# Projections with stationary weights: the high parts of two units, the low parts of all four, the high parts of the other two

## The chip, the cores and the metric

One Trainium2 chip, one NeuronCore of it. The metric is the device time of one execution in microseconds (us). Three runs of the kernel before gave 1080.13 us in the median (1079.92 to 1081.16).

## What is computed

One decoder layer on 256 tokens of width 2048, in float32. A combined input projection feeds 16 heads of sliding-window attention (window 128, two key/value heads, ALiBi, a learned sink per head) and 16 heads of forgetting attention ("FoX": the logit gets c[t] - c[s], where c is the running sum of log-sigmoid gates). Each group is RMS-normalised, one output projection follows, then a gated MLP with a causal convolution of width 3.

```python
h = rmsnorm(x, pre_mix_g)
q_a, k_a, v_a, q_b, k_b, v_b, f_b = split(h @ w_in)
o_a = swa_sink_attention(q_a, k_a, v_a, sinks)
o_b = forgetting_attention(q_b, k_b, v_b, log_sigmoid(f_b + b_forget))
x = x + rmsnorm(concat(rmsnorm(o_a), rmsnorm(o_b)) @ w_out, post_mix_g)
h = rmsnorm(x, pre_ffn_g)
gate, val = split(causal_dwconv(h @ w_up, conv_w, conv_b))
x = x + rmsnorm((gelu(gate) * val) @ w_down, post_ffn_g)
```

## The kernel before

Every float32 operand of a large product is split in two: a high part rounded to the matmul's float32r format and a low part with the rest. High x high, low x high and high x low are accumulated in PSUM. Weights come from HBM in units of 128 x 1024 numbers (512 KB). `w_load` starts the DMA into a tile `raw`, `w_split` has ScalarE (ACT) copy it into `whi` (line 111) and VectorE (DVE) subtract into `wlo` (line 114). `raw`, `whi` and `wlo` have five buffers each.

`proj_T` computes 256 output columns, transposed, with the weights stationary. The moving operand `hT` holds per row block the high part of the activations in columns 0 to 255 and the low part in 256 to 511. A high product (line 252) multiplies a 128 x 128 piece of `whi` with all 512 columns; a low product (line 257) multiplies a piece of `wlo` with the 256 high columns. The contraction of 2048 is 16 steps `kt`, four to a unit; each step is two products, one for each of the two PSUM banks. It is used 54 times: 3 times for queries of the sliding window, 8 times for queries and keys of FoX, 43 times in the MLP. Before, it takes the units in two passes of two: seven steps of high products, eight of low ones, the eighth of high ones.

TensorE's (PE's) instructions stand in the order of the code; a scheduler orders the other engines, whose queues run strictly in that order. The attention is woven into the projections by a clock of its own: `tick()` raises a counter and runs what `later(n, f)` had set for that count. `proj_T` ticks eight times; the value projections tick 12 times per block of columns, the output projection twice per unit. `attend` sets four pieces per pair of heads: `tables` (GpSimd, called POOL, fills the tile `p` with the bias), `scores` (12 products, line 441; DVE adds the bias and finds the minimum, line 447, ACT takes the exponential, line 459, DVE takes a reciprocal, line 463, and scales, line 466), `transposes` (6, line 476; ACT writes `ph`, DVE `pl`, lines 278 and 279), and `pv` with the weighted sum (lines 500 and 502 for FoX). They come at the ticks of

```python
def stages(n):
    return n, n + 6, n + 9
```

behind the call: for a FoX group `g` of two pairs, after its projection of queries and its projection of keys, `stages(3 + 8 * m)` for m = 0, 1. PSUM's eight banks are four of tag `acc` for projections and four of tag `att` for the attention. A pair's scores take two `att` banks, its transposes two, its weighted sum one. `p` has two buffers; `ph` and `pl` have one each. Keys of three pairs are kept.

Of the kernel before, what the change touches and what calls it, by code (L numbers as in the profile page):

```python
# [17 lines left out]
P = 128  # L18
# [4 lines left out]
KT = D // P  # L23
# [7 lines left out]
def hybrid_layer(ctx: ExitStack, tc: tile.TileContext, x, pre_mix_g, w_in, b_forget, sinks,  # L31
# [3 lines left out]
    pe, act, dve, pool, sp = nc.tensor, nc.scalar, nc.vector, nc.gpsimd, nc.sync  # L35
# [18 lines left out]
    def tick():  # L54
        now[0] += 1
        for f in todo.pop(now[0], []):
            f()
# [8 lines left out]
    def w_load(src, a, c, pin=False):  # L66
        raw = wp.tile([P, UNIT], F32, tag="raw", bufs=5, name="raw")
        i = sp.dma_start(raw[:, :a * c].rearrange("p (a c) -> p a c", a=a), src)
        if pin:
            tc.keep_in_program_order(i)  # L70
        return raw, a, c
# [4 lines left out]
    def w_parts(n, keep=None, still=False):  # L76


        if keep and keep[0] is None:
            return keep[1]  # L80
        if keep:
            return [keep[0].tile([P, UNIT], F32R, tag="h" + x, bufs=keep[1], name="w" + x)[:, :n]
                    for x in ("hi", "lo")]
        hi = wp.tile([P, UNIT], F32R, tag="whi", bufs=WB, name="whi")
        lo = wp.tile([P, UNIT + 128], F32R, tag="wlo", bufs=WB, name="wlo")
        c = LOW if still else 0
        return [hi[:, :n], lo[:, c:c + n]]
# [13 lines left out]
    def w_split(unit, pin=False, keep=None, begun=None, between=None, still=False):  # L101

        raw, a, c = unit
        n = a * c
        hi, lo = begun or w_parts(n, keep, still)
        for i in range(2 if between else 1):
            cs = slice(i * 512, i * 512 + 512) if between else slice(0, n)
            if i:
                between()
            if not between or i:  # L110
                i1 = act.copy(hi[:, cs], raw[:, cs])  # L111
                if pin:
                    tc.keep_in_program_order(i1)
            i2 = dve.tensor_tensor(lo[:, cs], raw[:, cs], hi[:, cs].bitcast(F32), op=ALU.subtract)  # L114
            if pin:
                tc.keep_in_program_order(i2)
        return [x.rearrange("p (a c) -> p a c", a=a) for x in (hi, lo)]
# [4 lines left out]
    def w_rows(w, k0, a, c0, c):  # L122
        return w[k0 * P:(k0 + a) * P, c0:c0 + c].rearrange("(a p) c -> p a c", p=P)
# [61 lines left out]
    hT = main.tile([P, KT, 512], F32R, tag="hT", name="hT")  # L185
# [55 lines left out]

    def proj_T(w, c0, banks):

        for v in (0, 2):
            parts = [w_split(w_load(w_rows(w, u * 4, 4, c0, 256), 4, 256), still=True)
                     for u in (v, v + 1)]
            steps = [(u, a) for u in range(2) for a in range(4)]

            def high(u, a):
                kt = (v + u) * 4 + a  # L250
                for m, b in enumerate(banks):
                    pe.matmul(b, parts[u][0][:, a, m * P:(m + 1) * P], hT[:, kt, :],  # L252
                              start=(kt == 0), stop=(kt == KT - 1))

            def low(u, a):
                for m, b in enumerate(banks):
                    pe.matmul(b[:, 256:512], parts[u][1][:, a, m * P:(m + 1) * P],  # L257
                              hT[:, (v + u) * 4 + a, 0:256], start=False, stop=False)

            for n, (u, a) in enumerate(steps[:-1]):  # L260
                high(u, a)
                if n in (2, 5):
                    tick()
            for n, (u, a) in enumerate(steps):
                low(u, a)
                if n == 4:
                    tick()
            high(*steps[-1])
            tick()

    def mm3(b, lhs, t, hi, lo, cols, first, last):

# [8 lines left out]
    with tc.tile_pool(name="mixp", bufs=1) as mp:  # L281
# [10 lines left out]
        def x_part(c, k2s, tag="att"):  # L292
            srcs = []
            for k2 in k2s:
                for j in range(2):
                    if tag == "acc" or j == 0:
                        tb = bank(tag)
                    kt = c * 4 + k2 * 2 + j
                    for t in range(2):
                        pe.transpose(tb[:, j * 256 + t * P:j * 256 + (t + 1) * P],  # L300
                                     x_in[:, t, kt * P:(kt + 1) * P], ident)
                    srcs.append((kt, tb[:, j * 256:(j + 1) * 256]))
            to_T(srcs, 0, 256, 0, True)
# [32 lines left out]
        for u in range(4):  # L336
            if u:
                parts = w_split(first[0][u], True, still=True)
            else:
                parts = w_split(first[0][u], True, begun=begun,  # L340
                                between=lambda: x_part(0, (1,), "acc"))
# [5 lines left out]
            parts = w_split(first[1][u], True, still=True)  # L347
# [238 lines left out]
        for g in range(4):  # L586
            if g == 0:
                b2 = bq0
            else:
                b2 = [bank(), bank()]  # L590
                proj_T(w_in, g * 256, b2)
            for m in range(2):
                swa_pair(2 * g + m, q_pair(b2[m]), stages(6 + 8 * (2 * g + m) - 8 * g))
# [3 lines left out]
        for p0, npair, cols in ((0, 3, 384), (3, 3, 384), (6, 2, 272)):  # L597
            b2 = [bank(), bank()]
            c0 = 3328 + p0 * P
            per = 3 if cols == 272 else 2  # L600
            for k0 in range(0, KT, per):
                na = min(per, KT - k0)
                hi, lo = w_unit(w_rows(w_in, k0, na, c0, cols), na, cols)
                for a in range(na):
                    kt = k0 + a
# [48 lines left out]
        for g in range(4):  # L654
            bq = [bank(), bank()]
            proj_T(w_in, 1280 + g * 256, bq)
            qs = [q_pair(b) for b in bq]
            bk = [bank(), bank()]
            proj_T(w_in, 2304 + g * 256, bk)
            for m in range(2):  # L660
                ki = (2 * g + m + 2) % NK
                k_pair(bk[m], ki)
                fox_pair(2 * g + m, qs[m], ki, stages(3 + 8 * m))
# [46 lines left out]
        hT = hT2  # L710
# [101 lines left out]
    with tc.tile_pool(name="ffn", bufs=1) as fp:  # L812
# [89 lines left out]
        for half in range(2):  # L902
            G = [fp.tile([P, 512], F32R, tag="G", bufs=FHALF, name=f"G{j}") for j in range(FHALF)]
            for g in range(FHALF // 2):
                c0 = (half * (FHALF // 2) + g) * 256
# [53 lines left out]
        def before_last(t, n):  # L959

            st = small.tile([P, 1], F32, tag="st", name="st_y")
            dve.tensor_reduce(st, ysq[t][:, 0:n], axis=AX.X, op=ALU.add)
            v = small.tile([P, 1], F32, tag="rv", name="rv")
            dve.tensor_scalar(v, st, 1.0 / D, EPS, op0=ALU.mult, op1=ALU.add)
            return v
# [32 lines left out]
        v = before_last(0, 3)  # L998
# [5 lines left out]
        for h in range(2):  # L1004
            if h:
                v = before_last(1, 4)
# [36 lines left out]
```

## Time and profile before

| | |
|---|---|
| time, median of 3 runs | 1080.13 us |
| the profiled execution: time, span | 1079.4 us, 1077.6 us |
| PE busy | 1064.9 us (99%) |
| DVE busy | 743.8 us (69%) |
| ACT busy | 619.4 us (57%) |
| POOL busy | 180.5 us (17%) |
| read from HBM | 199.58 MB, 187 GB/s with what is written |

The page gives busy time by engine over the whole span. Matmuls overlap in PE's pipeline, so one of 512 columns is listed with 392 ns, while its successor starts earlier; the distance between two starts says what one costs. A share of the whole run hides the stages; the stretch of one stage is read from the busy time by window.

### The profile page before, as it was taken

Reading aid. Unit: us, or ns where it says so; the run is one execution under the profiler, and the core shown is the slowest. Engines: PE = TensorE matmul, PEld = TensorE weight load, DVE = VectorE, ACT = ScalarE, POOL = GpSimd, SP = SyncE. Lnnn points to the kernel's source line nnn. Section 1 sums busy time; section 2 is a strip of 40 time slices with the busy share of each in tenths; the row PEclk is TensorE's granted clock in tenths of the full one; section 3 lists DMA queues with packets and bytes.
Section 4 is the critical chain, followed back from the end, with each engine's and each line's share of the span. In section 5 each row is a group of like instructions: output and inputs, shape, how many; then the busy total and the mean of one; then the engine's idle time right before and its main releaser. Section 6 shows DMA issues by size and latency. Waiting matters only on the chain.

```text
span 1077.6 us, 16247 instructions
## 1 busy us (share of the span) xinstructions
PE 1064.9 (99%) x5986; PEld 926.9 (86%) x5986; DVE 743.8 (69%) x1200; ACT 619.4 (57%) x1060; POOL 180.5 (17%) x252
## 2 busy tenths in 40 slices
PE   9999999999999999999999999999999999999996
PEld 7899988887889888888888888888888888888886
DVE  5988878887568876777677444457777777765563
ACT  7766766667557755656565443456565555644450
POOL 3343244332022201101010000001010100101111
PEclk9999999999999999999999999999999999999999
DMA  8645556544863765555665666665556656565652
GB/s 294 209 120 172 176 171 207 159 149 156 300 227 112 235 193 192 194 189 186 194 193 180 200 197 191 195 192 190 186 192 193 193 182 195 188 198 193 193 166 78
DMA packets 164970, 202.88 MB, mean 188 GB/s; under 512 B 6780, under 2 KB 130972, under 8 KB 164380
## 3 DMA queue, kind: packets, MB, share of 16 engines
q1 hardware_dynamic: 164176, 201.27, 58.3%
q8 instruction: 47, 0.77, 0.3%
q10 hardware_dynamic: 716, 0.58, 0.2%
q14 instruction: 31, 0.25, 0.1%
HBM read 199.58 MB, written 2.11 MB: 187 GB/s over the span
## 4 chain that ended last, share of the span: by engine, by line
PE 89%; DVE 4%; ACT 2%; POOL 2%; issue 2%; DMA 2%; SPq 0%; POOLq 0%; DVEq 0%; ACTq 0%
PE bank_acc L275 34%; PE bank_acc L252 19%; PE bank_att L252 14%; PE bank_acc L257 10%; PE bank_att L257 7%; DVE wlo L114 2%; POOL scr L408 1%; PE bank_att L441 1%; PE bank_acc L881 1%; ACT p L459 1%; PE bank_att L476 1%; DMA x_in<-in_x_dram 1%; PE bank_acc L877 0%; ACT whi L111 0%; DMA c_dram<-scr 0%
## 5 line engine op out<-in xcount | busy, mean ns | idle before, releaser
L114 DVE TENSOR_TENSOR wlo<-raw,whi 128x1024 fp32r<-128x1024 f32 (+3 forms) x357 | 454.2, 1275 | 246.8 <-ACT whi L111 173.6
L111 ACT CAST whi<-raw 128x1024 fp32r<-128x1024 f32 (+3 forms) x356 | 367.9, 1035 | 182.2 <-PE bank_acc L275 117.4
L252 PE MATMUL bank_acc<-hT,whi 128*128 128x512 f32 x1088 | 266.9, 392 | 0.0
L252 PEld LDWEIGHTS bank_acc<-hT,whi 128*128 128x128 f32 x1088 | 198.2, 188 | 37.3
L275 PE MATMUL bank_acc<-whi,G 128*128 128x512 f32 (+1 forms) x724 | 214.5, 378 | 0.0
L275 PEld LDWEIGHTS bank_acc<-whi,G 128*128 128x128 f32 x724 | 133.8, 188 | 25.6
L252 PE MATMUL bank_att<-hT,whi 128*128 128x512 f32 x640 | 154.2, 391 | 0.0
L848 POOL TENSOR_TENSOR u<-u,rowf 128x256 f32<-128x256 f32 x88 | 55.5, 653 | 538.3 <-DVE u L847 536.0
L257 PEld LDWEIGHTS bank_acc<-hT,wlo 128*128 128x128 f32 x1088 | 138.3, 189 | 5.7
L257 PE MATMUL bank_acc<-hT,wlo 128*128 128x256 f32 x1088 | 141.8, 281 | 0.0
L252 PEld LDWEIGHTS bank_att<-hT,whi 128*128 128x128 f32 x640 | 117.6, 188 | 22.7
L275 PE MATMUL bank_acc<-wlo,G 128*128 128x512 f32 (+1 forms) x362 | 137.1, 379 | 0.0
L257 PEld LDWEIGHTS bank_att<-hT,wlo 128*128 128x128 f32 x640 | 81.0, 189 | 3.1
L275 PE MATMUL bank_acc<-whi,oT 128*128 128x512 f32 (+1 forms) x272 | 82.5, 380 | 0.0
L257 PE MATMUL bank_att<-hT,wlo 128*128 128x256 f32 x640 | 82.0, 281 | 0.0
L275 PEld LDWEIGHTS bank_acc<-wlo,G 128*128 128x128 f32 x362 | 68.1, 188 | 12.7
L275 PEld LDWEIGHTS bank_acc<-whi,oT 128*128 128x128 f32 x272 | 50.2, 188 | 9.3
L275 PE MATMUL bank_acc<-wlo,oT 128*128 128x512 f32 (+1 forms) x136 | 51.2, 377 | 0.0
L275 PE MATMUL bank_acc<-whi,hT 128*128 128x384 f32 (+1 forms) x192 | 47.5, 323 | 0.0
L846 ACT COPY cs<-bank_acc 128x256 f32<-128x256 f32 x48 | 15.9, 372 | 52.2 <-PE bank_acc L252 52.2
L459 ACT ACTIVATE p<-p,nm 128x256 f32<-128x256 f32 (+1 forms) x64 | 28.4, 445 | 26.9 <-DVE nm L447 26.9
L846 ACT COPY cs<-bank_att 128x256 f32<-128x256 f32 x40 | 13.3, 373 | 47.2 <-PE bank_att L252 47.2
(200 smaller groups left out, 1016.4 us busy)
## 6 DMA issues: line engine op xcount, KB each, us to landing
raw<-in_w_up_dram SPq DMA_DIRECT2D x176, 512.0 KB, 3.5
raw<-in_w_down_dram SPq DMA_DIRECT2D x88, 512.0 KB, 4.6
raw<-in_w_in_dram SPq DMA_DIRECT2D x51, 512.0 KB, 4.1
raw<-in_w_out_dram SPq DMA_DIRECT2D x32, 512.0 KB, 4.7
raw<-in_w_in_dram SPq DMA_DIRECT2D x16, 384.0 KB, 3.4
cb<-c_dram SPq DMA_DIRECT2D x8, 256.0 KB, 3.6
x_sb<-in_x_dram SPq DMA_DIRECT2D x2, 1024.0 KB
raw<-in_w_in_dram SPq DMA_DIRECT2D x5, 408.0 KB, 3.2
```

Source lines behind the costliest of these rows:

```text
L111: i1 = act.copy(hi[:, cs], raw[:, cs])
L114: i2 = dve.tensor_tensor(lo[:, cs], raw[:, cs], hi[:, cs].bitcast(F32), op=ALU.subtract)
L252: pe.matmul(b, parts[u][0][:, a, m * P:(m + 1) * P], hT[:, kt, :], start=(kt == 0), stop=(kt == KT - 1))
L257: pe.matmul(b[:, 256:512], parts[u][1][:, a, m * P:(m + 1) * P], hT[:, (v + u) * 4 + a, 0:256], start=False, stop=False)
L275: pe.matmul(b, a, r[:, cols], start=(first and i == 0), stop=(last and i == 2))
L408: pool.tensor_tensor(dst, dst, row, op=ALU.mult)
L441: pe.matmul(sb[e][:, cs], a[r, t * P:(t + 1) * P], b[r, 0:nk], start=(n == 0), stop=(n == 2))
L459: act.activation(p[:, e, cs], p[:, e, cs], AF.Exp, bias=nm[:, t, e:e + 1], scale=-1.0, accum_out=rs[:, t, e:e + 1])
L476: pe.transpose(pb[:, i * P:(i + 1) * P], p[:, e, c:c + P], ident)
L846: act.copy(c, b[:, 256:512])
L848: pool.tensor_tensor(u[:, 2:258], u[:, 2:258], rowf, op=ALU.mult)
L881: pe.matmul(v(b), hi[:, ms], v(hT[:, kt, :]), start=(t == 0 and kt == 0), stop=False)
```

## The change

`proj_T` gets all four units in one pass: the high products of units 0 and 1, the low products of 0 and 1, those of 2 and 3, and the high products of 2 and 3. The loads and splits of units 2 and 3 are written behind the low products of units 0 and 1. It ticks four times, in steps 5 (high), 11 (low), 9 and 15 (high). Nothing else is changed: `stages`, the pools and the callers are as before. Line numbers behind it are 9 higher (2 to 3 inside it).

```diff
@@ -241,32 +241,41 @@
 
     def proj_T(w, c0, banks):
 
-        for v in (0, 2):
-            parts = [w_split(w_load(w_rows(w, u * 4, 4, c0, 256), 4, 256), still=True)
-                     for u in (v, v + 1)]
-            steps = [(u, a) for u in range(2) for a in range(4)]
-
-            def high(u, a):
-                kt = (v + u) * 4 + a
-                for m, b in enumerate(banks):
-                    pe.matmul(b, parts[u][0][:, a, m * P:(m + 1) * P], hT[:, kt, :],
-                              start=(kt == 0), stop=(kt == KT - 1))
-
-            def low(u, a):
-                for m, b in enumerate(banks):
-                    pe.matmul(b[:, 256:512], parts[u][1][:, a, m * P:(m + 1) * P],
-                              hT[:, (v + u) * 4 + a, 0:256], start=False, stop=False)
-
-            for n, (u, a) in enumerate(steps[:-1]):
-                high(u, a)
-                if n in (2, 5):
-                    tick()
-            for n, (u, a) in enumerate(steps):
-                low(u, a)
-                if n == 4:
-                    tick()
-            high(*steps[-1])
-            tick()
+
+        parts = {}
+
+        def get(*us):
+            for u in us:
+                parts[u] = w_split(w_load(w_rows(w, u * 4, 4, c0, 256), 4, 256), still=True)
+
+        def high(kt):
+            u, a = divmod(kt, 4)
+            for m, b in enumerate(banks):
+                pe.matmul(b, parts[u][0][:, a, m * P:(m + 1) * P], hT[:, kt, :],
+                          start=(kt == 0), stop=(kt == KT - 1))
+
+        def low(kt):
+            u, a = divmod(kt, 4)
+            for m, b in enumerate(banks):
+                pe.matmul(b[:, 256:512], parts[u][1][:, a, m * P:(m + 1) * P],
+                          hT[:, kt, 0:256], start=False, stop=False)
+
+        get(0, 1)
+        for kt in range(8):
+            high(kt)
+            if kt == 5:
+                tick()
+        for kt in range(8):
+            low(kt)
+        get(2, 3)
+        for kt in range(8, 16):
+            low(kt)
+            if kt == 11:
+                tick()
+        for kt in range(8, 16):
+            high(kt)
+            if kt in (9, 15):
+                tick()
 
     def mm3(b, lhs, t, hi, lo, cols, first, last):
```

On PE, an MLP projection and its neighbour, before (252 high, 257 low; a row with x16 is 16 products in a row):

```order
L252 MATMUL bank_att<-hT_3638,whi 128x512 x14
L257 MATMUL bank_att<-hT_3638,wlo 128x256 x16
L252 MATMUL bank_att<-hT_3638,whi 128x512 x16
L257 MATMUL bank_att<-hT_3638,wlo 128x256 x16
L252 MATMUL bank_att<-hT_3638,whi 128x512 x16
L257 MATMUL bank_att<-hT_3638,wlo 128x256 x16
L252 MATMUL bank_att<-hT_3638,whi 128x512 x16
L257 MATMUL bank_att<-hT_3638,wlo 128x256 x16
L252 MATMUL bank_att<-hT_3638,whi 128x512 x2
```

and now (254 high, 260 low):

```order
L254 MATMUL bank_att<-hT_3638,whi 128x512 x16
L260 MATMUL bank_att<-hT_3638,wlo 128x256 x32
L254 MATMUL bank_att<-hT_3638,whi 128x512 x32
L260 MATMUL bank_att<-hT_3638,wlo 128x256 x32
L254 MATMUL bank_att<-hT_3638,whi 128x512 x16
```

The step from low to high products stood twice in a projection and stands once.

On PE, in the FoX projections, where pairs of heads are woven in. Before, one pair at a time (the rows begin with the end of one pair's scores; 500 and 502 are a weighted sum, 476 are transposes):

```order
L441 MATMUL bank_att<-keys,qh 128x128 x2
L257 MATMUL bank_acc<-hT,wlo 128x256 x6
L252 MATMUL bank_acc<-hT,whi 128x512 x2
L500 MATMUL bank_att<-ph,vpb 128x512 x2
L500 MATMUL bank_att<-pl,vpb 128x512
L502 MATMUL bank_att<-ph,vpb 128x2x128 x2
L502 MATMUL bank_att<-pl,vpb 128x2x128
L252 MATMUL bank_acc<-hT,whi 128x512 x14
L257 MATMUL bank_acc<-hT,wlo 128x256 x16
L252 MATMUL bank_acc<-hT,whi 128x512 x8
L476 MATMUL bank_att<-ident,p 128x128 x6
L252 MATMUL bank_acc<-hT,whi 128x512 x8
```

Now, one place in the projection of queries of the last group (485 transposes, 450 scores, 12 rows of the run; the second pair's scores begin in the last row):

```order
L254 MATMUL bank_acc<-hT,whi 128x512 x28
L485 MATMUL bank_att<-ident,p 128x128 x12
L254 MATMUL bank_acc<-hT,whi 128x512 x4
L260 MATMUL bank_acc<-hT,wlo 128x256 x32
L254 MATMUL bank_acc<-hT,whi 128x512 x4
L450 MATMUL bank_att<-keys,qh 128x256 x2
L450 MATMUL bank_att<-keys,ql 128x256 x2
L450 MATMUL bank_att<-keys,qh 128x256 x2
L450 MATMUL bank_att<-keys,qh 128x128 x2
L450 MATMUL bank_att<-keys,ql 128x128 x2
L450 MATMUL bank_att<-keys,qh 128x128 x2
L450 MATMUL bank_att<-keys,qh 128x256 x2
```

and a little further in the same projection (the end of the second pair's scores, then 509 and 511, the weighted sums):

```order
L450 MATMUL bank_att<-keys,ql 128x128 x2
L450 MATMUL bank_att<-keys,qh 128x128 x2
L254 MATMUL bank_acc<-hT,whi 128x512 x12
L509 MATMUL bank_att<-ph,vpb 128x512 x2
L509 MATMUL bank_att<-pl,vpb 128x512
L511 MATMUL bank_att<-ph,vpb 128x2x128 x2
L511 MATMUL bank_att<-pl,vpb 128x2x128
L509 MATMUL bank_att<-ph,vpb 128x512 x2
L509 MATMUL bank_att<-pl,vpb 128x512
L511 MATMUL bank_att<-ph,vpb 128x2x128 x2
L511 MATMUL bank_att<-pl,vpb 128x2x128
L254 MATMUL bank_acc<-hT,whi 128x512 x16
```

Two pairs' transposes, scores and weighted sums stand side by side. This is so at three ticks for the transposes and weighted sums and at three for the scores.

On ACT, around one pair's softmax in the FoX stage, before (406 evacuates a projection's bank, 459 are exponentials, 278 writes `keys` and `ph`):

```order
L406 COPY scr<-bank_acc 128x256 x2
L111 CAST whi<-raw 128x1024
L278 CAST keys<-scr 128x256 x2
L278 CAST ph<-bank_att 128x384 x2
L111 CAST whi<-raw 128x1024
L459 ACTIVATE p,rs<-p,nm 128x256 x2
L459 ACTIVATE p,rs<-p,nm 128x128 x2
L111 CAST whi<-raw 128x1024
L511 ACTIVATE oT_126<-bank_att,gcol 64x256
L512 ACTIVATE sqo<-bank_att 64x256
```

and now, at the same place as the PE rows above (468 exponentials, 287 `keys` and `ph`, 415 evacuation):

```order
L111 CAST whi<-raw 128x1024
L287 CAST keys<-scr 128x256 x2
L111 CAST whi<-raw 128x1024
L287 CAST ph<-bank_att 128x384 x2
L111 CAST whi<-raw 128x1024
L468 ACTIVATE p,rs<-p,nm 128x256 x2
L468 ACTIVATE p,rs<-p,nm 128x128 x2
L468 ACTIVATE p,rs<-p,nm 128x256 x2
L468 ACTIVATE p,rs<-p,nm 128x128 x2
L111 CAST whi<-raw 128x1024
L415 COPY scr<-bank_acc 128x256 x2
L287 CAST ph<-bank_att 128x384 x2
```

The first `ph` row is that of one pair, the last that of the other pair whose transposes stood in the same tick; the exponentials of two further pairs, a weight copy and two evacuations stand between them.

## The prediction

> **What bounds the kernel.** I read the page first, then the busy time by stage, then the waits of TensorE.
>
> ```profile
> span 1077.6 us, 16247 instructions
> PE 1064.9 (99%) x5986; PEld 926.9 (86%) x5986; DVE 743.8 (69%) x1200; ACT 619.4 (57%) x1060; POOL 180.5 (17%) x252
> ```
> ```profile
> 72.70:128.50 55.80, 55.80 (x384) 54.11 (x383) 47.68 (x115) 37.52 (x88) 19.53 (x23) 1.00 0.51 157
> 168.80:240.80 72.00, 72.00 (x460) 63.07 (x459) 58.80 (x128) 47.91 (x113) 29.46 (x42) 1.00 0.54 166
> 400.00:500.00 100.00, 100.00 (x581) 88.38 (x579) 72.94 (x107) 59.24 (x91) 11.18 (x18) 1.00 0.59 190
> ```
> ```profile
> PE bank_att L441 <- ACT keys L278: 0.9, 1, 0.9
> PE bank_att L441 <- DVE keys L279: 0.8, 1, 0.8
> ACT whi L111 <- PE bank_acc L252: 30.4, 41, 2.7
> ACT whi L111 <- PE bank_att L252: 20.1, 29, 0.8
> ```
> The three stretches are the FoX value projections, the FoX projections and a piece of the MLP; the columns are length, then busy us of PE, weight loads, DVE, ACT and POOL, then granted clock, DMA share and GB/s. PE is full in all of them, so a microsecond in which PE waits is a microsecond of the end. After the start it waits twice in the whole run, 0.9 and 0.8 us, for keys. DVE is at 85% of the first stretch (47.68 of 55.80) and 82% of the second: little room there. The last two rows show ACT held up by PE: it wanted a weight buffer back that PE had not yet finished with, so weights are split ahead of use.
>
> **The change part by part.** *The order of products.* An MLP projection in the trace:
>
> ```profile
> 704.44 3.33 PE L252 MATMUL bank_acc<-hT,whi 128*128 128x512 f32 x14
> 707.61 2.05 PE L257 MATMUL bank_acc<-hT,wlo 128*128 128x256 f32 x16
> 709.50 3.81 PE L252 MATMUL bank_acc<-hT,whi 128*128 128x512 f32 x16
> 713.15 2.05 PE L257 MATMUL bank_acc<-hT,wlo 128*128 128x256 f32 x16
> ```
> From start to start: 14 high products 3.17 us, 226 ns each; 16 low ones 1.89 us, 118 ns each; 16 high ones behind low ones 3.65 us, 228 ns each. The last run is 0.03 us longer than 16 x 226 ns: that is what a step from low to high costs. A projection has two such steps before and one after. There are 11 projections of queries and keys and 43 in the MLP: 54 x 0.03 = 1.6 us gained; I take 1.5. A step from high to low costs nothing to be seen.
>
> The Trainium skill, "TensorE: Matmul & The Clock Gate", section "Back-to-back issue gap", gives a warm gap of N/2.4 + 2.5 ns whatever stands beside it, 216 ns at 512 columns; the trace has 226 here, and the gap depends on the neighbour. By that rule this term is zero and the sum is 1.5 us higher.
>
> *Low parts are needed earlier.* Unit 2's low part is now read behind 16 high and 16 low products, 16 x 0.226 + 16 x 0.118 = 5.5 us into a projection, and was at 8.7. High parts of units 2 and 3 are held to the end, so the next projection's fourth unit gets its buffer when unit 2 lets go, halfway into the last run, at 9.2 us, and has until 11.1 + 6.4 = 17.5 us for a copy and a subtraction (1.05 + 1.3 us by the rows below). Loads move with the splits, four per projection as before; five raw buffers and a DMA share of 0.59 hide them. I cost all this at nothing in the MLP, where DVE is at 73%. If the cover went, PE would wait at the first low product of unit 2 or 3.
>
> *Half the ticks.* A projection called `tick` eight times and now calls it four times; `stages` is unchanged. A FoX pair's scores come 3 or 11 ticks behind its group. With 16 ticks to a group no two pairs met; with 8, tick 11 of one group is tick 3 of the next. So pair X (second of a group) and pair Y (first of the next) now issue their scores in one tick, their transposes in one tick and their weighted sums in one tick. Three times this hits tiles that exist once. The transposes of X and Y take all four `att` banks. X's are split at once, but `ph` and `pl` have one buffer, so Y's two banks stay full until X's weighted sum has read `ph`. In between the next two pairs' scores are due: four banks, with two free. The prices, from one stretch of the FoX stage and one of the output projection:
>
> ```profile
> 186.60 0.65 POOL L549 TENSOR_SCALAR p<-cb,cq 128x256 f32<-128x256 f32 x1
> 186.96 0.85 ACT L278 CAST ph<-bank_att 128x384 fp32r<-128x384 f32 x2
> 187.47 1.02 DVE L279 TENSOR_TENSOR pl<-bank_att,ph 128x384 fp32r<-128x384 f32 x2
> 187.70 1.06 ACT L111 CAST whi<-raw 128x1024 fp32r<-128x1024 f32 x1
> 190.29 0.41 DVE L447 CUSTOM_DVE_ANT_0 p<-bank_att,p 128x256 f32<-128x256 f32 x1
> 190.75 0.51 ACT L459 ACTIVATE p<-p,nm 128x256 f32<-128x256 f32 x1 [1.99 <-DVE nm L447]
> 190.98 0.28 DVE L447 CUSTOM_DVE_ANT_0 p<-bank_att,p 128x128 f32<-128x128 f32 x1
> 191.19 0.28 DVE L447 CUSTOM_DVE_ANT_0 p<-bank_att,p 128x128 f32<-128x128 f32 x1
> 192.42 0.19 ACT L459 ACTIVATION_READ_ACCUMULATOR p<-p,nm 128x1 f32 x1
> 192.64 0.18 DVE L463 RECIPROCAL rs<-rs 128x4 f32<-128x4 f32 x1 [1.16 <-ACT p L459]
> 192.86 1.01 DVE L466 TENSOR_SCALAR p<-p,rs 128x256 f32<-128x256 f32 x4
> 193.78 1.22 DVE L114 TENSOR_TENSOR wlo<-raw,whi 128x1024 fp32r<-128x1024 f32 x1
> 196.78 0.65 ACT L406 COPY scr<-bank_acc 128x256 f32<-128x256 f32 x2 [0.61 <-PE bank_acc L252]
> ```
> ```profile
> 255.34 2.73 PE bank_acc L275 x12
> 258.07 0.84 PE bank_att L441 x12
> 260.48 0.69 PE bank_att L500 x3
> 261.17 0.35 PE bank_att L502 x3
> ```
> Read: four reductions 1.2 us (190.29 to 191.47), a bank free after the third (0.97); four exponentials 1.86 us (190.75 to 192.61), reciprocal and scaling 1.2; 12 products, a tick or two, 2.73; scores 0.84; a weighted sum 1.04.
>
> Collision A, in the projection of queries of the last group, counted from the first score of X. X's scores end at 0.84, its reductions run 1.05 to 2.25. Y's scores need X's two banks: they start at 2.1 and end at 3.15, 1.45 late. DVE has X's reciprocal and scaling queued ahead of Y's reductions, so these run 4.7 to 5.9 behind X's exponentials (to 3.4). The older pair's weighted sum, 12 products later at 5.9, finds its bank free and ends at 6.95. Its partner needs `ph` rewritten, and on ACT that copy stands behind Y's exponentials (to 7.0), a weight copy (8.1), two evacuations (8.75): done at 9.6, a wait of 2.65. On DVE `pl` stands behind Y's scaling and a weight subtraction, done at 10.6; its reader is due at 10.05, another 0.55. Sum 4.7 us. Queued behind each wait are only projection products; what waits for them is the next evacuation.
>
> Collision B, at the start of the output projection, has only 12 products (2.73 us) between transposes and scores, where A has 5.6. The same walk gives 0.4 (`pl` frees X's banks late), 2.0, 1.25 (weighted sum, since only six products follow the scores), 2.2 and 1.2: 7.1 us. Collision C has one pair's scores: only the `ph` and `pl` waits, 2.1 + 1.2 = 3.3 us. Together 15.1 us.
>
> These are durations of one quiet stretch. With group means,
>
> ```profile
> L447 DVE CUSTOM_DVE_ANT_0 p<-bank_att,p 128x256 f32<-128x256 f32 x16 | 6.1, 414 | 0.0
> L459 ACT ACTIVATE p<-p,nm 128x256 f32<-128x256 f32 x32 | 16.1, 503 | 26.9 <-DVE nm L447 26.9
> L459 ACT ACTIVATION_READ_ACCUMULATOR p<-p,nm 128x1 f32 x64 | 12.0, 187 | 0.0
> L114 DVE TENSOR_TENSOR wlo<-raw,whi 128x1024 fp32r<-128x1024 f32 x333 | 430.8, 1295 | 242.3 <-ACT whi L111 169.4 <-issue 30.5 <-PE bank_acc L257 23.4
> ```
> laid end to end without overlap of a reading with the next operation (four exponentials near 2.5 us, four reductions 1.7), the same walks give 7.2, 9.6 and 4.5: 21.3 us. The floor, whatever stands in the queues, is three reductions before Y's scores (A, B: about 1.2 more than now) and `ph` plus half of `pl` between two weighted sums (0.85 + 0.5, three times): 6.5 us. I take 17, near the quiet stretch, since it is this very sequence.
>
> *More sliding-window pairs in the value projections.* Pairs now come two in 12 ticks there instead of one in 8, so six scores fall into that stage where four did. A pair costs PE 2.2 us, DVE at least 1.2 + 0.2 + 1.0 + 1.0 for softmax and `pl`, and for its output
>
> ```profile
> L496 DVE TENSOR_TENSOR scr<-bank_att,olow 64x256 f32<-64x256 f32 x16 | 6.6, 415 | 1.9 <-ACT olow L493 1.7
> L513 DVE SCALAR_TENSOR_TENSOR oT<-scr,gcol,oT 128x256 fp32r<-128x256 f32 x8 | 5.6, 697 | 0.0
> ```
> 2 x 0.42 + 0.7: near 5 us. The stage becomes 60.2 us of PE with 57.7 us of DVE, 96%. DVE's in-order waits were 8.1 us of this stage; if all of them stay, it overruns by up to 5.6 us, less what it is ahead. Between 0 and 6 I take 1.5, because all five weight buffers can be full when the stage begins.
>
> *Keys.* Scores follow the key projection by 16 high, 32 low and 4 high products (8.3 us) or more, where 14 high and 10 low did; the first of the two old waits goes, and B holds the second: -1.7.
>
> **Sum**, against the profiled execution (span 1077.6, time 1079.4; the median of three runs is 0.7 above it): -1.5 + 17 + 1.5 - 1.7 = +15.3, so 1094.7, or 1095 against the median.
>
> **Rivals.** *No wait in PE.* The faster engines come round in time, and only -3.2 us is left: 1077. The place is the second weighted sum of a tick; it decides if the three collisions cost under 1.1 us each, while `ph` alone is 0.85 behind the first sum. Against it: the queue on ACT. Chance 0.04, and 0.03 for a standstill.
>
> *DVE bounds the value projections*: the overrun is 6 us rather than 1.5, 1100 to 1103. For it: 85% before, two pairs more. Against it: the buffers are full when the stage begins. 0.16.
>
> *The clock falls.* Before warming up, PE is slow:
>
> ```profile
> 1.26 2.74 PE L168 MATMUL bank_acc<-junk 128*128 128x512 bf16 x6 [1.26 <-DVE junk L163]
> ```
> six products at about 0.43 us against 0.226. If a wait of 2 to 3 us in A, B and C closes the gate, and reopening takes about those 2.7 us at half pace, each costs 1.3: 4 us, 1099. The trace shows no wait so long with a warm clock, so nothing speaks against it but the length. 0.10. The Trainium skill, same page, Part 1 on the clock gate, puts the idle window at about 3.4 us; no run here shows it.
>
> *Queues are kinder than their order suggests*: the floor of 6.5 us, 1083 to 1088. 0.14.
>
> **The numbers.** The forecast, 1089 to 1100, has 0.53. 1085 to 1105 leaves out the two cases without a wait and the far ends of two others. A measurement of this kernel tells 0.2%, 2.2 us, from no change: faster 0.04, same 0.03, slower 0.93.
>
> **What would show it.** After: two-score ticks whose second scores wait for DVE's reductions; waits of the second weighted sum for ACT `ph` and DVE `pl`, three of each, 1 to 3 us; PE under 99% between some 140 and 270 us and full in the MLP; 54 fewer steps from low to high; DVE at 95% or more in the value projections. Wrong would be a row of waits for `wlo` in the MLP, or PE without a wait in the FoX stage.

## Result, and the profile after

The changed kernel takes 1095.07 us in the median (1094.63 to 1095.61), the kernel before, beside it on the same chip, 1080.45 us. The ratio is 1.0132, 95% interval 1.0121 to 1.0144: 14.6 us slower, where 1095 us was forecast. The number came out; two of the terms behind it did not, and they nearly cancelled.

The page of the changed kernel: span, busy time by engine, and the granted clock of TensorE in 40 slices.

```profile
span 1093.9 us, 16259 instructions
PE 1071.4 (98%) x5986; PEld 932.5 (85%) x5986; DVE 743.2 (68%) x1200; ACT 612.5 (56%) x1060; POOL 222.9 (20%) x252
PEclk9999999998999999999999999999999999999999
```

DVE and ACT do the work they did before. PE shows 6.5 us more busy time for the same 5986 products, and one slice has an 8 in the row of the clock. Both say that PE was not only kept waiting: for some of the time it also ran slower.

What PE waited for, over the whole run: us in total, times, longest.

```profile
PE bank_att L509 <- ACT ph L287: 4.1, 3, 1.6
PE bank_att L450 <- ACT p L468: 3.5, 2, 2.2
PE bank_att L509 <- DVE pl L288: 1.3, 2, 0.9
...
PE bank_att L497 <- DVE pl L288: 1.2, 1, 1.2
...
PE bank_att L509 <- ACT p L468: 0.9, 1, 0.9
PE bank_att L497 <- ACT ph L287: 0.6, 1, 0.6
```

Lines 509 and 497 are the weighted sums of FoX and of the sliding window, 450 the scores. Three second weighted sums wait for ACT's `ph`, two scores for a bank of the pair ahead of them: the walk through collisions A, B and C, in those places. Two rows (497) had no place in the walk: a sliding-window pair in the value projections. The waits for `keys` are gone, and there is no row for `wlo`. All these waits together are 11.6 us. (For the two waits of line 450 the profile names ACT `p` as the releaser; in the queues it is DVE's reductions of X that free the banks.)

Busy time by window (length, then PE, weight loads, DVE, ACT and POOL, then granted clock, DMA share, GB/s): the value projections, the FoX projections, a piece of the MLP, and then three short windows at half clock, each with the window ahead of it.

```profile
72.70:132.90 60.20, 58.39 (x403) 55.70 (x399) 53.74 (x143) 42.95 (x108) 21.64 (x28) 0.97 0.50 148
168.80:240.80 72.00, 69.84 (x432) 60.59 (x429) 53.98 (x123) 44.16 (x102) 25.66 (x33) 0.98 0.57 172
400.00:500.00 100.00, 100.00 (x580) 88.49 (x579) 73.88 (x110) 57.34 (x90) 19.98 (x18) 1.00 0.62 190
```
```profile
125.97:129.38 3.41, 1.65 (x11) 1.11 (x9) 3.34 (x10) 3.38 (x5) 1.09 (x2) 1.00 0.00 0
129.39:132.80 3.41, 3.37 (x14) 3.28 (x15) 3.00 (x4) 1.79 (x5) 0.00 (x0) 0.50 0.80 213
218.14:221.54 3.40, 2.13 (x26) 1.78 (x25) 1.20 (x8) 1.73 (x8) 1.02 (x3) 1.00 0.27 95
221.55:224.95 3.40, 3.40 (x9) 2.63 (x9) 2.29 (x13) 1.77 (x9) 0.00 (x0) 0.50 0.82 281
252.28:255.67 3.39, 1.29 (x6) 0.98 (x6) 2.19 (x14) 3.31 (x11) 0.00 (x0) 1.00 0.00 0
255.69:262.50 6.81, 6.12 (x15) 4.53 (x16) 3.69 (x7) 3.17 (x9) 1.46 (x2) 0.50 0.27 77
```

The MLP is full and at full clock. In the windows the pattern is the same three times: PE is busy for 1.3 to 2.1 us of a stretch of 3.41 us, and in the next stretch of that length its clock is at half (in B for two of them). PE was busy for 12.9 of these 13.6 us at half clock, so about 6.4 us of work were lost, which fits the 6.5 us by which its busy time grew.

From the first product of a stage to the first of the next, in us (work moves between the four woven stages, so their sum is what compares):

| | before | after | order, 8 ticks | old order, 4 ticks | pairs apart | waits filled | second ph, pl | put together |
|---|---|---|---|---|---|---|---|---|
| sliding-window projections | 40.18 | 35.47 | 40.63 | 35.50 | 35.45 | 35.47 | 35.47 | 40.70 |
| value projections | 55.67 | 63.80 | 55.69 | 62.22 | 63.74 | 62.26 | 63.74 | 55.69 |
| FoX projections | 110.11 | 107.99 | 112.10 | 109.43 | 106.98 | 108.07 | 103.46 | 103.57 |
| output projection | 90.63 | 105.73 | 89.46 | 106.45 | 93.26 | 103.47 | 95.10 | 95.07 |
| sum of the four | 296.59 | 312.99 | 297.88 | 313.60 | 299.43 | 309.27 | 297.77 | 295.03 |
| MLP projections | 477.26 | 475.86 | 475.83 | 477.26 | 475.86 | 475.86 | 475.86 | 475.86 |

The four woven stages grew by 16.4 us. Waits account for +11.6 - 1.7 (the old ones for keys), the clock for +6.4, the order of products in 11 projections for about -0.3: 16.0, and 0.4 us are not accounted for. The MLP gained 1.40 us. The start, which waits for the input, took 33.60 us instead of 32.32 in this execution, so its span is 16.3 us longer, while the medians differ by 14.6.

### The profile page after: what moved, and what is told of

Its sections match the earlier page's. It is cut to its first block, busy times and chain, and to the rows that moved or that the text cites. A ratio compares the mean times of both kernels' runs of the same rounds, so it can differ in the third digit from the quotient of the medians.

```text
span 1093.9 us, 16259 instructions
## 1 busy us (share of the span) xinstructions
PE 1071.4 (98%) x5986; PEld 932.5 (85%) x5986; DVE 743.2 (68%) x1200; ACT 612.5 (56%) x1060; POOL 222.9 (20%) x252
## 4 chain that ended last, share of the span: by engine, by line
PE 96%; DVE 1%; ACT 1%; issue 1%; POOL 0%; DMA 0%; SPq 0%; DVEq 0%; POOLq 0%; ACTq 0%
PE bank_acc L284 34%; PE bank_acc L254 23%; PE bank_att L254 13%; PE bank_acc L260 12%; PE bank_att L260 7%; PE bank_att L450 1%; PE bank_att L485 1%; PE bank_att L220 1%; PE bank_acc L890 1%; PE bank_acc L220 1%; ACT p L468 1%; PE bank_acc L886 0%; DVE wlo L114 0%; PE bank_att L509 0%; DMA x_in<-in_x_dram 0%
## 5 line engine op out<-in xcount | busy, mean ns | idle before, releaser
L114 DVE TENSOR_TENSOR wlo<-raw,whi 128x1024 fp32r<-128x1024 f32 (+3 forms) x357 | 435.2, 1229 | 254.5 <-ACT whi L111 247.7
L111 ACT CAST whi<-raw 128x1024 fp32r<-128x1024 f32 (+3 forms) x356 | 363.6, 1035 | 275.0 <-issue 131.1
L254 PE MATMUL bank_acc<-hT,whi 128*128 128x512 f32 x1088 | 260.2, 393 | 0.0
L254 PEld LDWEIGHTS bank_acc<-hT,whi 128*128 128x128 f32 x1088 | 201.9, 189 | 40.3
L857 POOL TENSOR_TENSOR u<-u,rowf 128x256 f32<-128x256 f32 x88 | 97.1, 1125 | 496.2 <-DVE u L856 489.2
L254 PE MATMUL bank_att<-hT,whi 128*128 128x512 f32 x640 | 150.5, 390 | 0.0
L260 PEld LDWEIGHTS bank_acc<-hT,wlo 128*128 128x128 f32 x1088 | 132.9, 189 | 2.8
L260 PE MATMUL bank_acc<-hT,wlo 128*128 128x256 f32 x1088 | 134.1, 281 | 0.0
L284 PEld LDWEIGHTS bank_acc<-wlo,G 128*128 128x128 f32 x362 | 68.1, 188 | 12.9
L417 POOL TENSOR_TENSOR scr<-scr 128x256 f32<-128x256 f32 x26 | 28.1, 1098 | 80.6 <-DVE scr L416 74.7
L859 ACT ACTIVATE yg<-u,cw 128x256 f32<-128x256 f32 x44 | 26.5, 603 | 27.8 <-POOL u L857 27.8
```

The lines of the kernel that those rows point to most:

```text
L284: pe.matmul(b, a, r[:, cols], start=(first and i == 0), stop=(last and i == 2))
L417: pool.tensor_tensor(dst, dst, row, op=ALU.mult)
L857: pool.tensor_tensor(u[:, 2:258], u[:, 2:258], rowf, op=ALU.mult)
L859: act.activation(y, u[:, 2:258], AF.Identity, bias=cw[:, 3, ch:ch + 1], scale=cw[:, 2, ch:ch + 1])
```

## Experiments

Each kernel is compared with runs of the kernel before on the same chip. Clock and waits are those of its profiled execution.

### The order and the ticks, one at a time

Edit of the first, against the changed kernel:

```diff
-            if kt == 5:
+            if kt in (2, 5):
...
+            if kt == 2:
+                tick()
...
-            if kt == 11:
+            if kt in (8, 13):
...
-            if kt in (9, 15):
+            if kt in (9, 12, 15):
```

> The new order of products with eight ticks to a projection, as before. My theory (the four ticks cost it all, by bringing pairs together; the order by itself gains 54 steps x 0.03 us): 1078.9 us, ratio 0.9985, MLP shorter by 1.4 us, PE at full clock and no wait of over 1 us behind the start. Rival (the order itself costs, since the low parts of all four units are wanted early and buffers are let go late): about 1095, or at least some us over 1080.5.

Measured: 1079.22 us, ratio 0.9988 (0.9979 to 0.9997). Its MLP is 1.43 us shorter than before. One wait is left behind the start, and behind it stands a window at half clock (first the row of the waits, then that of the window):

```profile
PE bank_att L452 <- ACT keys L289: 1.7, 1, 1.7
```
```profile
163.94:167.34 3.40, 3.40 (x20) 3.28 (x21) 2.76 (x10) 3.40 (x9) 0.00 (x0) 0.50 0.87 300
```

The wait was 1.65 us long and ended at 163.3. The forecast of this run was right in the time and in the MLP, and wrong in its last clause: in the profiled execution there is a wait of over 1 us, and the clock is not full. That execution (1080.94 us) is the second longest of the eleven, nine of which lie between 1078.4 and 1079.8; whether those have the window is not known. The order by itself costs nothing and gains about 1 us.

Edit of the second, against the kernel before:

```diff
-                if n in (2, 5):
+                if n == 5:
                     tick()
...
-                if n == 4:
-                    tick()
```

> The old order of products with four ticks to a projection (behind the sixth high step and at the end of each pass). My theory: the same three collisions of pairs and the sliding-window pair in the value projections, so 1095.07 + 1.5 = about 1096.5 us (1094 to 1099, since the ticks stand a few products elsewhere), with waits for ph and pl and the clock at half in one to three windows. Rival (the new order needs low parts early, the ticks alone are harmless): 1080.5.

Measured: 1097.57 us, ratio 1.0156 (1.0142 to 1.0170), as forecast. The clock is at half in four windows, where one to three were expected. The waits are those of the changed kernel at the same work (line 498 is the FoX weighted sum, 439 the scores, 486 the sliding window's):

```profile
PE bank_att L498 <- ACT ph L276: 3.7, 3, 1.6
PE bank_att L439 <- ACT p L457: 3.3, 2, 2.0
PE bank_att L498 <- DVE pl L277: 2.7, 3, 0.9
...
PE bank_att L486 <- DVE pl L277: 1.2, 1, 1.2
```

Together the two runs settle the first question: the loss belongs to the ticks, all of it, and the new order gains what its steps from low to high were counted to be worth.

### Pairs that do not meet

```diff
-                fox_pair(2 * g + m, qs[m], ki, stages(3 + 8 * m))
+                fox_pair(2 * g + m, qs[m], ki, stages(3 + 4 * m))
```

> The changed kernel, with the FoX pairs of a group 4 ticks apart rather than 8, so that with 8 ticks to a group no two pairs issue in one tick. My theory: the three collisions go (9.9 us of waits) and with them the two stretches of half clock that stand in A and B (about 5 us, part of it inside the waits); the wait in the value projections with its half clock (3.5 us) stays, and so do the gains: 1080 to 1083 us. Rival (the FoX stages have too much work per tick whatever meets; DVE and ACT are the bound there): 1092 or more.

Measured: 1080.71 us, ratio 1.0004 (0.9996 to 1.0013), at the low end of the theory. With four ticks, and the FoX pairs' work in the same two stages (one pair's scores move from the output projection into the FoX projections), the three collisions are gone; what remains of the list is the sliding-window pair (line 497) and two half microseconds. The last row is the window behind that pair's wait.

```profile
PE bank_att L497 <- DVE pl L288: 1.2, 1, 1.2
...
PE bank_att L497 <- ACT ph L287: 0.6, 1, 0.6
```
```profile
129.10:132.50 3.40, 3.22 (x13) 3.12 (x14) 3.14 (x5) 1.82 (x4) 0.00 (x0) 0.50 0.78 200
```

So it is the meeting that cost, not the load of the stage. The eleven times of this kernel form two groups, 1079.8 to 1080.7 (six, mean clock 0.997 to 0.998) and 1081.9 to 1082.2 (five, clock 0.996 in each), 1.9 us apart. One window at half clock is 1.7 us; the profiled execution, of the second group, has one. That the first group has none is inferred from its mean clock, since only the profiled one shows its windows. The kernel before has such groups too: of its 21 executions on that chip four took 1081.6 to 1081.8 us at a mean clock of 0.996, the others 1079.8 to 1081.1 at 0.997 or 0.998. So a median that moves by a tenth of a per cent may only tell how often such a window falls.

### Is the half clock a cost of its own?

In the changed kernel, products of a junk tile stand where PE waits:

```diff
+        def fill(n, b=None):
+            if n and b is None:
+                b = bank()
+            for _ in range(n):
+                pe.matmul(b, junk[:, 0:P], junk, start=True, stop=True)
...
             def scores():
+                fill({12: 5, 14: 9}.get(j, 0))
...
                 o = bank("att")
+                fill({5: 7, 10: 10, 12: 7, 14: 7}.get(j, 0), o)
```

> The changed kernel, with 45 junk products of 512 bf16 columns put on TensorE where it waits (ahead of the second scores of a tick and of second weighted sums, in the value projections, A, B and C); nothing reads their results. Theory that the half clock is answer to the waits and costs by itself: the records show full clock behind the start, and the time falls by some 5 us to about 1090 (1.7 in the value projections, 3.4 in B, nothing in A, where the wait for ph grows by what the products behind it gain). Rival (the half clock costs nothing, since what it slows would wait anyhow): 1095 with a full clock. Rival (the clock falls for another reason than idle time): the same half clock, 1095 or more.

Measured: 1091.35 us, ratio 1.0099 (1.0085 to 1.0113). The four places, in windows of the profiled execution:

```profile
119.00:134.00 15.00, 14.46 (x101) 12.47 (x102) 13.92 (x36) 11.46 (x26) 4.76 (x6) 1.00 0.49 144
218.14:229.00 10.86, 10.48 (x57) 7.66 (x57) 8.22 (x26) 7.63 (x25) 2.31 (x2) 1.00 0.48 152
245.00:263.00 18.00, 15.93 (x81) 11.23 (x80) 10.06 (x36) 11.80 (x32) 3.92 (x7) 1.00 0.29 84
270.00:280.00 10.00, 9.02 (x41) 6.41 (x41) 6.32 (x13) 6.65 (x14) 1.48 (x2) 1.00 0.23 75
```

The clock is full in all four, and the kernel is 3.7 us faster for 45 products more (1095.07 - 1091.35, on two chips; by the ratios 0.33% of 1080, 3.6 us). So idle time is what closed the clock, and the closed clock cost by itself. It is less than the 5 us expected; where a fill overshot its wait it may have added time, which was not measured.

### Is it the one buffer of ph and pl?

For the four pairs whose weighted sum comes second in a tick, `ph` and `pl` get a second place. `oall` is oT as one tile; the rows used are written later, and hT is free once the projections end.

```diff
-                st["h"] = ap.tile([P, 2, 384], F32R, tag="ph", name="ph")
-                st["l"] = ap.tile([P, 2, 384], F32R, tag="pl", name="pl")
+                if j in (5, 10, 12):
+                    st["h"], st["l"] = oall[:, 14:16, 0:384], oall[:, 12:14, 0:384]
+                elif j == 14:
+                    st["h"], st["l"] = hT[:, 0:2, 0:384], hT[:, 2:4, 0:384]
+                else:
+                    st["h"] = ap.tile([P, 2, 384], F32R, tag="ph", name="ph")
+                    st["l"] = ap.tile([P, 2, 384], F32R, tag="pl", name="pl")
```

> The changed kernel, with a second place for ph and pl (in rows of oT and hT that lie idle) for the four pairs whose weighted sum comes second in a tick (j = 5, 10, 12, 14); ticks and order as in the changed kernel. Theory that the one buffer of ph and pl makes the second weighted sums wait: their waits go (1.8 us in the value projections, 0.9 in A, 2.1 in B, 2.5 in C, together 7.3), and the half clock in the value projections and B with them (1.7 + 3.4); the waits for banks by the second scores (1.3 in A, 2.2 in B) stay: 1083 to 1086 us. Rival (the copies into ph and pl are late because ACT and DVE have too much queued, whatever buffer they fill): the same waits, 1092 to 1095.

Measured: 1078.79 us, ratio 0.9982 (0.9973 to 0.9990), 4 us under the range. What PE still waits for behind the start:

```profile
PE bank_att L503 <- DVE oall L288: 1.2, 1, 1.2
PE bank_att L491 <- DVE oall L528: 1.0, 1, 1.0
...
PE bank_att L503 <- ACT oall L287: 0.6, 1, 0.6
```

In A, B and C the waits for `ph` and `pl` are gone, as the theory said. The scores' waits, which the expectation had left standing, are gone as well: a transposed pair that can be split at once also gives its two banks back at once, so the next scores find four free. Ticks, order and load are those of the changed kernel; one buffer made the difference of 16 us (1095.07 to 1078.79, on two chips; by the ratios 1.50%). That `oT` is one tile there was not tried alone. The middle row is new, the last three of twelve transposes waiting at their turn.

And the theory failed in one place: the sliding-window pair (line 503) waits 0.6 + 1.2 us as it did, though it has its own buffer now. In the changed kernel, the timeline of ACT and that of DVE there (start, length, engine, line, operation, and idle time before it):

```profile
123.86 0.51 ACT L468 ACTIVATE p<-p,nm 128x256 f32<-128x256 f32 x1 [1.72 <-DVE nm L456]
...
125.73 1.03 ACT L111 CAST whi<-raw 128x1024 fp32r<-128x1024 f32 x1
126.79 0.86 ACT L287 CAST ph<-bank_att 128x384 fp32r<-128x384 f32 x2
```
```profile
126.27 1.04 DVE L475 TENSOR_SCALAR p<-p,rs 128x256 f32<-128x256 f32 x4
127.23 1.21 DVE L114 TENSOR_TENSOR wlo<-raw,whi 128x1024 fp32r<-128x1024 f32 x1
128.37 1.01 DVE L288 TENSOR_TENSOR pl<-bank_att,ph 128x384 fp32r<-128x384 f32 x2
```

PE transposed the pair at 123.3 and wanted `ph` at 127.1. ACT takes it behind the next pair's four exponentials (from 123.86, themselves late by 1.72 us for DVE) and a weight copy, DVE takes `pl` behind that pair's scaling and a weight subtraction. Here it is the queue, not the buffer.

### Two versions that missed

The first moves the third of eight ticks 14 low products later, and the four behind it by less, to be rid of the wait for keys.

```diff
-            if kt == 2:
-                tick()
...
-            if kt in (8, 13):
+            if kt in (9, 13):
...
-            if kt in (9, 12, 15):
+            if kt in (8, 10, 13, 15):
```

> The new order with eight ticks, but the third 14 low products later (steps 2 and 5 high, 9 and 13 low, 8, 10, 13 and 15 high). The run with eight ticks showed one wait of 1.65 us for keys with the clock at half for 3.4 us behind it. Theory (scores came too soon behind the keys): that wait and the half clock go, 1.65 + 1.7 us less: 1076 to 1077 us, faster than the kernel before by 0.3%. Rival (the keys are late for a queue that moves along with the ticks, or the wait is one run's accident): 1079.

Measured: 1083.02 us, ratio 1.0016 (1.0006 to 1.0026). The wait at 162 us is gone, and others for keys have come at the last group, at 217 and at 245 to 247 us:

```profile
PE bank_att L450 <- DVE keys L288: 1.7, 2, 0.9
PE bank_att L450 <- ACT keys L287: 1.7, 1, 1.7
```

Neither number held, and 1083 is above both. The mechanism of the rival fits (the keys came late again where the scores had moved), but which instruction ahead of the keys makes the difference was not followed up. Behind the waits at 245 to 247 us there is again a window at half clock, from 248.66 to 252.07.

The second gives the sliding-window pairs even distances too:

```diff
-                swa_pair(2 * g + m, q_pair(b2[m]), stages(6 + 8 * (2 * g + m) - 8 * g))
+                swa_pair(2 * g + m, q_pair(b2[m]), stages(6 + 6 * (2 * g + m) - 4 * g))
...
-                fox_pair(2 * g + m, qs[m], ki, stages(3 + 8 * m))
+                fox_pair(2 * g + m, qs[m], ki, stages(3 + 4 * m))
```

> The changed kernel (four ticks) with the FoX pairs 4 ticks apart and the sliding-window pairs 6 apart instead of 4 and 8 in turn. With the FoX pairs alone apart, 0.6 + 1.2 us of waits and one window of half clock were left in the value projections. Theory: both go, 1.8 + 1.7 us less than 1080.7: 1077 to 1078. Rival (DVE is the bound in the value projections, which now hold two pairs more than in the kernel before): the loss stays there, 1080 or more.

Measured: 1083.16 us, ratio 1.0020 (1.0009 to 1.0030). The rival held in its number: in the profiled execution the loss stays around that stage, as a wait of 2.1 us for the last pair's sums, and two windows at half clock behind it, in which DVE is busy 6.71 of 6.81 us. That execution (1085.43 us) is one of the three longest of twelve; five took 1081.5 to 1082.1 us, and their windows are not known. That DVE is the bound there is not shown: over 72.70 to 135.00 us it is busy for 51.23 of 62.30.

```profile
PE bank_att L450 <- DVE scr L505: 2.1, 1, 2.1
```
```profile
133.16:139.97 6.81, 6.39 (x23) 5.24 (x24) 6.71 (x21) 6.39 (x18) 0.91 (x1) 0.50 0.69 227
```

### Put together

New order, second place for `ph` and `pl`, four ticks in the FoX projections, and eight in those of the sliding window, so that the value projections hold the pairs they held before (the edit against the version with the second place; the conditions of the eight ticks are left out):

```diff
-    def proj_T(w, c0, banks):
+    def proj_T(w, c0, banks, eight=False):
...
-                proj_T(w_in, g * 256, b2)
+                proj_T(w_in, g * 256, b2, True)
...
-                if j in (5, 10, 12):
+                if j in (10, 12):
```

> A version put together from the runs so far: the new order, eight ticks in the three sliding-window projections (so that these pairs stand in the value projections as in the kernel before), four ticks in the FoX projections, and a second place for ph and pl (j = 10, 12, 14). The run with the second place had 0.6 + 1.2 us of waits and one window of half clock (1.7 us) left in the value projections. Theory (that wait is DVE's and ACT's load by six pairs' scores there instead of four): both go, 1078.8 - 3.5 = about 1075.5 us, faster than the kernel before by 0.4 to 0.5%. Rival (the work left out there comes back as waits in FoX, as it did with the pairs 6 ticks apart): 1078 to 1080.

Measured: 1077.25 us (1076.66 to 1077.93), ratio 0.9966 (0.9954 to 0.9979): faster than both kernels, 3.6 us under the one before, and between the theory's number and the rival's. The waits in the value projections and the half clock are gone:

```profile
72.70:129.10 56.40, 56.40 (x386) 54.61 (x385) 49.12 (x118) 38.89 (x92) 18.90 (x22) 1.00 0.52 155
240.00:255.00 15.00, 14.00 (x70) 11.46 (x71) 11.11 (x36) 12.84 (x34) 5.76 (x10) 1.00 0.36 112
```

The second row holds the one wait of over 0.2 us left behind the start, 1.0 us ahead of transposes. The expectation of 1075.5 was taken from the other version's median less 3.5 us, but part of that version's executions lie in a lower group (1078.2 to 1078.8, the rest 1079.9 to 1080.4), which by the groups above would be those without the half clock; their mean clocks do not tell (0.995 to 0.998 in the lower group, 0.995 to 0.997 in the other). Against its profiled execution (1079.97), which has a window at half clock, this one's (1077.12) is 2.9 us shorter, where 3.5 was expected.

## Why the prediction was right, and where it was not

**The order of products, -1.5.** Right. The MLP gained 1.40 us in 43 projections, 0.033 each, and the run with the old order has the old MLP length to 0.01 us. So the rule by which this term is zero did not hold here. The Trainium skill, "TensorE: Matmul & The Clock Gate", section "Back-to-back issue gap", calls that formula the gap of an isolated product. Here the products stand in a stream, at 226 ns each.

**Low parts earlier, nothing.** Right: no wait for `wlo` anywhere, and the MLP's PE stays at 100.00 of 100.00 us.

**Half the ticks, +17.** The mechanism was right in its places, its order and its cause: with pairs apart it is gone, with a second place for `ph` and `pl` it is gone. The size of the term was wrong: PE idled 9.8 us in A, B and C. Of the 7.2 us too much, 1.9 is the choice of 17 over the 15.1 of the walk. A was walked at 1.45 + 2.65 + 0.55 and measured as 1.27 + 0.89 + 0; B at 7.1 and measured at 5.2; C at 3.3 and measured at 2.5. The miss in A has a cause that can be read in the timelines of the changed kernel, PE's and then ACT's:

```profile
218.93 0.28 PE L450 MATMUL bank_att<-keys,qh 64*128 64x128 f32 x2
220.48 0.51 PE L450 MATMUL bank_att<-keys,qh 64*128 64x256 f32 x2 [1.27 <-ACT p L468]
...
221.44 4.60 PE L254 MATMUL bank_acc<-hT,whi 128*128 128x512 f32 x12
225.88 0.62 PE L509 MATMUL bank_att<-ph,vpb 128*128 128x512 f32 x2
...
227.98 0.73 PE L509 MATMUL bank_att<-ph,vpb 128*128 128x512 f32 x2 [0.89 <-ACT ph L287]
```
```profile
227.06 0.86 ACT L287 CAST ph<-bank_att 128x384 fp32r<-128x384 f32 x2 [0.43 <-PE bank_att L511]
```

The scores of X began at 218.30. `ph` was forecast to be done 9.6 us behind that, and was, at 227.92. But the 12 products ahead took 4.44 us from start to start instead of 2.73, mostly in the window at half clock, and so PE came to the wait 1.8 us later. The wait was measured shorter because the clock had already taken the time. That `ph` was on time is in part luck: the walk had ACT busy until then, while ACT was free 0.43 us earlier and waited for the older sum (line 511), slowed by the clock, to let the buffer go.

**The value projections, +1.5.** Forecast as DVE's load, 95% or more; DVE was at 53.74 of 60.20, 89%. Measured: 1.8 us of wait and 1.7 of half clock, in one place, from the order in two queues. The step that took DVE's summed work and its waits for what overruns was the wrong one; this was a fourth place where two pairs stood too close.

**Keys, -1.7.** Right; both waits are gone.

**The clock, nothing, and a rival at 0.10.** Wrong: this is the step that failed. The prediction held against the rival only that no wait so long had been seen with a warm clock, and asked for waits of 2 to 3 us in A, B and C. Pauses of 1.3 to 2.1 us within one window were enough; the clock fell in the value projections, in A and twice in B, and not in C; and the four half windows cost 6.4 us, where the rival had three times 1.3. The Trainium skill, "TensorE: Matmul & The Clock Gate", Part 1, gives a free-running window of 3413 ns. The trace agrees on the grid: the three half stretches start at 129.39, 221.55 and 255.69 us, 27 and 10 times 3.413 us apart. The condition that the Trainium skill gives there, an idle window of about 3.4 us, is not what this trace shows, where PE was busy for 1.3 to 2.1 us of the window ahead.

**The sum.** Waits were forecast at 17 + 1.5 = 18.5 us and the clock at 0; measured were 11.6 and 6.4, which is 18.0. That this agrees to half a microsecond is chance, though not all of it: in A the two were the same microseconds, and a walk at full clock puts into the wait what the chip put into the clock. The run with filled waits has none of the half clock and came to 1091.35, so a forecast right in every step would have had some 11 us of net loss without the clock's part and 3.7 for that.

Of the signs that the prediction named, the two-score ticks, the waits for `ph` (0.9 to 1.6 us) and the full MLP were there; second sums waited for `pl` two times in FoX, not three; DVE at 95% was not there. PE was at 94% between 140 and 270 us, but the kernel before is under 99% there too (128.25 of 130.00 us), so that sign says less than it seemed to.

**Not settled.** The put-together version and that with the second place are 0.5 and 1.2 us shorter in the woven stages than waits, clock and order account for; what else their meeting pairs save was not taken apart.

## What to carry to other kernels

A counter that paces woven work is part of the schedule: halving its ticks left every distance in the code as it was and halved the products between two pieces, and pairs that had never met shared single buffers. Before counting the engines' load, look for the tile that exists once and ask who holds its PSUM banks meanwhile; a second place of 6 KB per partition was worth 16 us here. And where waits of more than a microsecond come together, price the clock too.

## What the hardware showed unexpectedly

TensorE's clock went to half after far shorter pauses than expected, and by windows on a fixed grid, so that the same pause may cost or not. A pause of 0.58 + 1.18 us inside one window was followed by half clock, and one of 1.65 us; in the run with the old order and four ticks the first of these, 0.58 + 1.24 us, was split between two windows and was not. In B 1.54 us of pause lay in a window and the next was still full; in A 1.27 us, with only scores (64 rows of weights) beside it, was enough. In C, 1.05 and 1.46 us of pause lay in two windows in a row, and both were followed by full clock. Over all ten profiled executions, between the start and the last product, a window at full clock was followed by half clock where PE was busy for 1.29 to 1.78 us of its 3.4, and in A's place (2.13, and 2.12 in the run with the old order and four ticks); apart from these, windows with 1.87 us or more were not. What exactly the window counts is not settled by these.

POOL's product on `u` in the MLP (line 848 before, 857 now) became much slower for the same shape. The first row is of the kernel before, the second of the changed one: busy us and mean ns stand behind the bar.

```profile
L848 POOL TENSOR_TENSOR u<-u,rowf 128x256 f32<-128x256 f32 x88 | 55.5, 653 | 538.3 <-DVE u L847 536.0 <-DVE rowf L831 2.3
```
```profile
L857 POOL TENSOR_TENSOR u<-u,rowf 128x256 f32<-128x256 f32 x88 | 97.1, 1125 | 496.2 <-DVE u L856 489.2 <-DVE rowf L840 7.0
```

It goes with the order of products, not the ticks (1097 ns with the new order and eight ticks, 667 with the old one and four). POOL is not on the path in the MLP, so it cost nothing. The two traces show what goes with it. In the changed kernel every second product of this line begins about 0.14 us behind the start of a weight subtraction on DVE (line 114), and takes 1.62 us, ending 0.50 us behind the subtraction; the others take 0.64. In the kernel before, POOL's product begins 0.13 us ahead of the subtraction and takes 0.64 us, and the subtraction takes 1.59 us instead of 1.22. So of the two, the one that begins second is held up; this was read from the traces, not tested by a run.
